# Seven block products instead of eight for half of the contraction in the gate and up projections

## The chip, the cores and the metric

The program runs on one core of a Trainium2 chip. The metric is the time of one execution on the device in microseconds. The kernel before took 1974.96 us, the median of three runs (1974.09 to 1976.55). About 0.2% of that, some 4 us, is what a measurement of this kernel can tell from no change.

Engines are named as in the profile: PE (TensorE, matrix products), PEld (its loads of the stationary operand), DVE (VectorE), ACT (ScalarE), POOL (GpSimd), SP (SyncE, which here only issues transfers). Each runs its own queue in order.

## What is computed

One decoder layer on 256 tokens of width 2048, all in float32: a SwiGLU half step, a mixer (dilated attention and gated linear attention), cross-attention into 256 memory tokens, and a second SwiGLU half step. The change concerns the two half steps:

```python
def swiglu(h, w_gate, w_up, w_down):
    return (jax.nn.silu(h @ w_gate) * (h @ w_up)) @ w_down
...
        x = x + 0.5 * swiglu(rms_norm(x, ffn1_norm[l]), ffn1_w_gate[l], ffn1_w_up[l], ffn1_w_down[l])
...
        x = x + 0.5 * swiglu(rms_norm(x, ffn2_norm[l]), ffn2_w_gate[l], ffn2_w_up[l], ffn2_w_down[l])
```

`w_gate` and `w_up` are 2048 x 5632, `w_down` is 5632 x 2048. The root-mean-square factor of a token is applied after the products, as a scale of a row; the gain vector is multiplied into the tokens before.

## The kernel before

**Three products for one.** TensorE multiplies float32r operands here. To keep float32 accuracy each operand is split exactly into two 12-bit parts, high and low, and a product becomes three: high times high, high times low, low times high (`mm3`, lines 130 to 136).

**Tiles.** The 256 tokens are two tiles of 128 (t = 0, 1). The contraction runs over 16 k tiles of 128, four of which make a group: a group of weights is 128 partitions x 4 x 512, one megabyte, one transfer. A chunk f is 512 columns of `w_gate` and of `w_up`; there are 11 chunks in a half step. A matrix product instruction has a 128x128 block of the tokens as its stationary operand and 512 weight columns as the moving one; the result adds into a PSUM bank of 128 x 512 (pool `acc`, four banks).

**Weights on their way.** `wgroup` (lines 108 to 127) loads a group into a buffer `raw` (three of them) from SP's queue, and hands it on in halves of two k tiles: ACT writes the high part `wh` (line 125), DVE the low part `wl = raw - wh` (line 126). There are four buffers each for `wh` and `wl` (`WB = 4`), so the split of a half can begin once PE has finished with the half four before it. `proj` (line 138) runs over the groups; each half feeds 12 matrix products, two k tiles x two token tiles x three.

**A chunk.** `ffn` (line 228): gate projection, then `sg = silu(r * acc)` on ACT (line 250), up projection, then `h = r * acc * sg` on DVE (line 256). `h` is transposed by PE into `tp` (line 239, eight transposes) and split again into `hTh`, `hTl` (lines 157 and 158). After all 11 chunks the down projection runs over four chunks of 512 output columns, each over all 11 groups.

**What sets the order.** The source is a Tile program: a scheduler puts the instructions of each engine into a fixed order when the program is built, by priority (weight splits have a raised one, `WPRI`) and by its own estimates, and derives all semaphores. `later(n, fn)` puts work off by n halves of a projection. Buffers come from pools; an instruction that needs a buffer waits until the last reader of its former content is done. In the pool `up` (`UB = 44` buffers of 2 KB per partition) lie the split h, and most tiles of the mixer.

## Time and profile before

| | |
|---|---|
| runs | 1974.96 us median of three, 1974.09 to 1976.55 |
| profiled execution, span | 1974.5 us; its page gives no other time of its own, and the span lies inside the range of the runs |
| one gate and up chunk (58.06 to 102.48 us) | 44.42 us |
| PE busy | 1966.5 us, 100% of the span |
| DVE busy | 1039.2 us, 53% |
| ACT busy | 912.3 us, 46% |
| POOL busy | 61.2 us, 3% |
| DMA engines | 52.2% busy for the queue of the loads, 370.74 MB |
| TensorE clock granted | 0.999 of full speed |

A busy share is the time in which at least one instruction of the engine was in execution; PE's instructions overlap, so that 0.39 us of one matrix product is not the time after which the next may start. An "idle before" is the time an engine stood still before instructions of a group, and the name behind the arrow is what ended it. The two half steps' gate and up chunks lie at 14 to 502 us and from about 1289 us on, each followed by a down projection; mixer and cross-attention lie between.

### The profile page before, as it was taken

Reading aid. Unit: us, or ns where it says so; the run is one execution under the profiler, and the core shown is the slowest. Engines: PE = TensorE matmul, PEld = TensorE weight load, DVE = VectorE, ACT = ScalarE, POOL = GpSimd, SP = SyncE. Lnnn points to the kernel's source line nnn. Section 1 sums busy time; section 2 is a strip of 40 time slices with the busy share of each in tenths; the row PEclk is TensorE's granted clock in tenths of the full one; section 3 lists DMA queues with packets and bytes.
Section 4 is the critical chain, followed back from the end, with each engine's and each line's share of the span. In section 5 each row is a group of like instructions: output and inputs, shape, how many; then the busy total and the mean of one; then the engine's idle time right before and its main releaser. Section 6 shows DMA issues by size and latency. Waiting matters only on the chain.

```text
span 1974.5 us, 22181 instructions
## 1 busy us (share of the span) xinstructions
PE 1966.5 (100%) x9000; PEld 1632.6 (83%) x9000; DVE 1039.2 (53%) x1102; ACT 912.3 (46%) x1115; POOL 61.2 (3%) x61
## 2 busy tenths in 40 slices
PE   9999999999999999999999999999999999999999
PEld 7888888888888888778888889888888888888887
DVE  6455444444455545546785566654444444444443
ACT  6444444444444436444576446544444444433332
POOL 2000000000000000002230000000000000000000
PEclk9999999999999999999999999999999999999999
DMA  8555555555555554445465554455555555555553
GB/s 308 187 191 189 192 192 192 187 188 187 189 190 190 195 204 149 171 156 201 172 219 204 196 186 154 173 192 192 188 187 188 188 189 190 191 192 202 203 204 116
DMA packets 57683, 374.26 MB, mean 190 GB/s; under 512 B 6475, under 2 KB 7627, under 8 KB 13932
## 3 DMA queue, kind: packets, MB, share of 16 engines
q1 hardware_dynamic: 56428, 370.74, 52.2%
q10 hardware_dynamic: 1152, 2.10, 0.3%
q8 instruction: 70, 1.15, 0.2%
q14 instruction: 33, 0.27, 0.0%
HBM read 370.72 MB, written 2.10 MB: 189 GB/s over the span
## 4 chain that ended last, share of the span: by engine, by line
PE 99%; DMA 0%; SPq 0%; DVE 0%; ACT 0%; POOL 0%; issue 0%; POOLq 0%
PE acc L136 32%; PE acc L134 32%; PE acc L135 32%; PE tp L239 1%; PE tp L198 1%; DMA xr<-in_xT_dram 0%; PE dsp L475 0%; PE op L492 0%; PE op L496 0%; PE tp L582 0%; PE sc L595 0%; PE op L629 0%; PE sc L738 0%; PE op L773 0%; PE tp L616 0%; PE zp L409 0%
## 5 line engine op out<-in xcount | busy, mean ns | idle before, releaser
L126 DVE TENSOR_TENSOR wl<-raw,wh 128x1024 fp32r<-128x1024 f32 (+1 forms) x690 | 845.6, 1227 | 855.5 <-ACT wh L125 855.1
L125 ACT CAST wh<-raw 128x1024 fp32r<-128x1024 f32 (+1 forms) x690 | 724.8, 1052 | 965.5 <-PE acc L136 944.6
L134 PE MATMUL acc<-wh,xTh 128*128 128x512 f32 x1824 | 714.8, 392 | 1.8 <-ACT wh L125 1.8
L135 PE MATMUL acc<-wl,xTh 128*128 128x512 f32 x1824 | 710.9, 390 | 1.0 <-DVE wl L126 1.0
L136 PE MATMUL acc<-wh,xTl 128*128 128x512 f32 x1824 | 710.7, 390 | 0.0
L134 PEld LDWEIGHTS acc<-wh,xTh 128*128 128x128 f32 x1824 | 342.5, 188 | 73.6 <-ACT wh L125 3.0
L135 PEld LDWEIGHTS acc<-wl,xTh 128*128 128x128 f32 x1824 | 343.0, 188 | 72.7 <-DVE wl L126 2.5
L136 PEld LDWEIGHTS acc<-wh,xTl 128*128 128x128 f32 x1824 | 342.8, 188 | 71.5
L134 PE MATMUL acc<-wh,hTh 128*128 128x512 f32 x704 | 274.3, 390 | 0.0
L136 PE MATMUL acc<-wh,hTl 128*128 128x512 f32 x704 | 273.9, 389 | 0.0
L135 PE MATMUL acc<-wl,hTh 128*128 128x512 f32 x704 | 273.9, 389 | 0.0
L136 PEld LDWEIGHTS acc<-wh,hTl 128*128 128x128 f32 x704 | 132.1, 188 | 27.5
L134 PEld LDWEIGHTS acc<-wh,hTh 128*128 128x128 f32 x704 | 132.1, 188 | 27.4
L135 PEld LDWEIGHTS acc<-wl,hTh 128*128 128x128 f32 x704 | 132.2, 188 | 27.2
L134 PE MATMUL acc<-wh,mTh 128*128 128x512 f32 x128 | 50.1, 392 | 0.0
L136 PE MATMUL acc<-wh,mTl 128*128 128x512 f32 x128 | 49.8, 389 | 0.0
L135 PE MATMUL acc<-wl,mTh 128*128 128x512 f32 x128 | 49.8, 389 | 0.0
L250 ACT ACTIVATE sg<-acc,r 128x512 f32<-128x512 f32 x44 | 30.1, 687 | 6.1 <-PE acc L136 6.1
L134 PE MATMUL acc<-wh,memh 128*128 128x256 f32 (+1 forms) x96 | 31.4, 327 | 0.0
L256 DVE SCALAR_TENSOR_TENSOR h<-acc,r,sg 128x512 f32<-128x512 f32 x44 | 30.9, 743 | 0.0
L136 PE MATMUL acc<-wh,meml 128*128 128x256 f32 (+1 forms) x96 | 30.6, 318 | 0.0
L135 PE MATMUL acc<-wl,memh 128*128 128x256 f32 (+1 forms) x96 | 30.5, 318 | 0.0
(249 smaller groups left out, 801.3 us busy)
## 6 DMA issues: line engine op xcount, KB each, us to landing
raw<-in_ffn_w_up_dram SPq DMA_DIRECT2D x88, 1024.0 KB, 4.8
raw<-in_ffn_w_down_dram SPq DMA_DIRECT2D x88, 1024.0 KB, 4.8
raw<-in_ffn_w_gate_dram SPq DMA_DIRECT2D x85, 1024.0 KB, 4.8
raw<-in_w_in_dram SPq DMA_DIRECT2D x48, 1024.0 KB, 4.8
raw<-in_w_out_dram SPq DMA_DIRECT2D x16, 1024.0 KB, 4.8
raw<-in_xattn_w_k_dram SPq DMA_DIRECT2D x4, 1024.0 KB, 4.7
raw<-in_xattn_w_q_dram SPq DMA_DIRECT2D x4, 1024.0 KB, 4.7
raw<-in_xattn_w_v_dram SPq DMA_DIRECT2D x4, 1024.0 KB, 4.9
```

What stands on the lines that cost most here:

```text
L125: SC.copy(wh[:, d], src)
L126: V.tensor_sub(wl[:, d], src, wh[:, d].bitcast(F32))
L134: PE.matmul(acc[t], lh, wh, start=first and i == 0, stop=False)
L135: PE.matmul(acc[t], lh, wl, start=False, stop=False)
L136: PE.matmul(acc[t], ll, wh, start=False, stop=last and i == len(half) - 1)
L198: PE.transpose(tp[:, j], src[:, t, j * P:(j + 1) * P], ident)
L239: PE.transpose(tp[:, j], hs[t][:, j * P:(j + 1) * P], ident)
L250: SC.activation(s, acc[t], AF.Silu, scale=r[:, t:t + 1])
L256: V.scalar_tensor_tensor(h, acc[t], r[:, t:t + 1], sg[t], op0=ALU.mult, op1=ALU.mult)
```

## The change

For 10 of the 11 chunks of each half step (all but f = 0), half of the contraction is done by seven block products instead of eight (`seven`, new). The 2 x 2 blocks are: the tokens' t = 0 and 1 by k-tile groups 0 and 1, times the weights' groups 0 and 1 by gate and up. The old way needs eight products of a token block (128 x 512) with a weight group (512 x 512): two tokens, two groups, two matrices. The new one has seven, each of 12 matrix products (four k tiles x three parts). Here they are P1 to P7 in program order, with the weight that each one splits:

- P1: gate group 0 + gate group 1 (`b11` after the first sum)
- P2: gate group 1 (`b21`)
- P3: gate group 0 + gate group 1 + up group 0 (`b11` after the second sum)
- P4: up group 1 (`b22`)
- P5: all four (`b11` after the third sum)
- P6: up group 0 (`b12`)
- P7: up group 0 + gate group 0 (`b12` after its sum)

Of the four weight sums two are made by a transfer that adds what it brings onto the buffer (`add_hbm`, issued from POOL's queue: `b11` before P1, `b12` between P6 and P7), two by DVE on the whole group of 128 x 2048 (`add`). Five differences of token blocks stand on the other side; they are made once in a half step (`differences`), on POOL, split by ACT and DVE. Intermediate sums are taken out of PSUM (`s21`, `s22`, `s12`: copies on ACT, and four additions or subtractions of 128 x 512 on DVE in a chunk). The other half of the contraction, groups 2 and 3, stays as it was (`plain`): U2 and U3 of up between P6 and P7, then G2 of gate, P7, G3. The halves of each are called a and b.

Every weight block of the seven is split anew, so that a chunk has 11 group splits instead of 8. All four PSUM banks of `acc` are in use during a chunk: Y, Z, X, R.

Buffers: `raw` five instead of three, `UB` 34 instead of 44, `SB` 8 instead of 6. So that 34 do, a half step is done in two segments, chunks 0 to 5 and 6 to 10, each with its own part of the down projection, which is added to the running x.

```diff
-UB = 44
-SB = 6
+UB = 34
+SB = 8
+RB = 5
+SEGS = (range(0, 6), range(6, NF))
...
-                raw = wp.tile([P, kn, n], F32, tag="raw", name="raw")
+                raw = wp.tile([P, kn, n], F32, tag="raw", name="raw", bufs=RB)
...
+    def parts(raw):
+        for h in range(2):
+            with tc.high_priority(WPRI):
+                wh = wp.tile([P, 2, 512], F32R, tag="wh", name="wh", bufs=WB)
+                wl = wp.tile([P, 2, 512], F32R, tag="wl", name="wl", bufs=WB)
+                src = raw[:, 2 * h:2 * h + 2]
+                SC.copy(wh, src)
+                V.tensor_sub(wl, src, wh.bitcast(F32))
+            yield [(2 * h + kk, wh[:, kk], wl[:, kk]) for kk in range(2)]
+
+    def add(dst, src):
+        with tc.high_priority(WPRI):
+            V.tensor_add(dst, dst, src)
+
+    def add_hbm(dst, src):
+        with tc.high_priority(WPRI):
+            G.dma_start(dst, src, accum_op=ALU.add)
+
+    def mms(bank, form, half, start, stop):
+        hi, lo = form
+        for i, (k, wh, wl) in enumerate(half):
+            PE.matmul(bank, hi[:, k], wh, start=start and i == 0, stop=False, skip_group_check=True)
+            PE.matmul(bank, hi[:, k], wl, start=False, stop=False, skip_group_check=True)
+            PE.matmul(bank, lo[:, k], wh, start=False, stop=stop and i == len(half) - 1, skip_group_check=True)
+
+    def product(bank, form, raw, start):
+        for h, half in enumerate(parts(raw)):
+            mms(bank, form, half, start and h == 0, h == 1)
+            tick()
+
+    def plain(banks, forms, raw, start, order):
+        for h, half in enumerate(parts(raw)):
+            for t in order:
+                mms(banks[t], forms[t], half, start[t] and h == 0, h == 1)
+            tick()
+
+    def differences():
+        x = {}
+        for c in range(2):
+            for t in range(TT):
+                x[t, c] = U([P, 4, P], F32, "xf")
+                hi, lo = (p[:, :, t * P:(t + 1) * P].bitcast(F32) for p in xT[c])
+                G.tensor_tensor(x[t, c], hi, lo, op=ALU.add)
+        r = {}
+        for name, a, b in (("22-21", (1, 1), (1, 0)), ("12-21", (0, 1), (1, 0)), ("22-12", (1, 1), (0, 1)),
+                           ("21-11", (1, 0), (0, 0)), ("11-12", (0, 0), (0, 1))):
+            d = W2([P, 4, P], "d")
+            G.tensor_tensor(d, x[a], x[b], op=ALU.subtract)
+            hi = U([P, 4, P], F32R, "Fh")
+            lo = U([P, 4, P], F32R, "Fl")
+            SC.copy(hi, d)
+            V.tensor_sub(lo, d, hi.bitcast(F32))
+            r[name] = (hi, lo)
+        return r
+
+    def seven(W1, W2_, f, F, A12, A21, rest):
+        Y, Z, X, R = [pa.tile([P, 512], F32, tag="acc", name="acc") for _ in range(4)]
+        b11 = load(W1, f, 0)
+        b21 = load(W1, f, 1)
+        add_hbm(b11, W1[f, 1])
+        product(Y, A21, b11, True)
+        s21 = W2([P, 512], "s21")
+        SC.copy(s21, Y)
+        b12 = load(W2_, f, 0)
+        product(Z, F["22-21"], b21, True)
+        add(b11, b12)
+        product(Y, F["12-21"], b11, False)
+        s22 = W2([P, 512], "s22")
+        SC.copy(s22, Y)
+        b22 = load(W2_, f, 1)
+        product(X, F["22-12"], b22, True)
+        add(b11, b22)
+        product(R, A12, b11, True)
+        V.tensor_sub(s22, R, s22)
+        product(Y, F["21-11"], b12, False)
+        add_hbm(b12, W1[f, 0])
+        s12 = W2([P, 512], "s12")
+        SC.copy(s12, Y)
+        for g in (2, 3):
+            plain((R, X), (rest(0, g), rest(1, g)), load(W2_, f, g), (False, False), (1, 0))
+        V.tensor_sub(s12, R, s12)
+        V.tensor_add(s22, X, s22)
+        plain((Y, Z), (rest(0, 2), rest(1, 2)), load(W1, f, 2), (False, False), (1, 0))
+        product(Y, F["11-12"], b12, False)
+        plain((Y, Z), (rest(0, 3), rest(1, 3)), load(W1, f, 3), (False, False), (0, 1))
+        V.tensor_add(s21, Z, s21)
+        return Y, s21, s12, s22
...
-        for f in range(NF):
-            acc = proj(wg, f, lhs_x, range(4), fine if f == 0 else None)
...
+        for seg in SEGS:
+            for f in seg:
+                if f == 0:
+                    acc = proj(wg, f, lhs_x, range(4), fine)
+                    if callable(r):
+                        r = r()
+                    F = differences()
+                else:
+                    y, s21, s12, s22 = seven(wg, wu, f, F, x_block(0, 1), x_block(1, 0), x_block)
+                    acc = [y, s21]
...
+            for c in range(NC):
+                acc = proj(wd, c, lhs_h, seg, last=last and final and c == NC - 1)
```

(`load`, also new, is the transfer of one group into a `raw` buffer from SP's queue, line 164 of the changed file.)

**DVE.** Line numbers of the rows below are those of each file; a row with x14 stands for 14 in a row. Before, from the middle of one chunk to the middle of the next:

```order
L126 TENSOR_TENSOR wl<-raw,wh 128x1024 x14
L256 SCALAR_TENSOR_TENSOR h<-acc,r_333,sg 128x512 x2
L126 TENSOR_TENSOR wl<-raw,wh 128x1024 x2
L158 TENSOR_TENSOR hTl<-tp,hTh 128x512 x2
L126 TENSOR_TENSOR wl<-raw,wh 128x1024 x14
```

Now, from the end of chunk 4 on. The first row's five splits are P7b, G3a and G3b of chunk 4 and P1a and P1b of chunk 5; then comes the first weight sum on DVE (L180), P2a, the addition from Z (L257), the first h (L372), P2b and P3a, the second h, P3b, the first split of the transposed h (L262), P4a and the second weight sum:

```order
L175 TENSOR_TENSOR wl<-raw,wh 128x1024 x5
L180 TENSOR_TENSOR raw<-raw 128x2048
L175 TENSOR_TENSOR wl<-raw,wh 128x1024
L257 TENSOR_TENSOR s_1541<-acc,s_1541 128x512
L372 SCALAR_TENSOR_TENSOR s_1653<-s_1653,r_333,sg 128x512
L175 TENSOR_TENSOR wl<-raw,wh 128x1024 x2
L372 SCALAR_TENSOR_TENSOR s_1586<-s_1586,r_333,s_1541 128x512
L175 TENSOR_TENSOR wl<-raw,wh 128x1024
L262 TENSOR_TENSOR hTl<-tp,hTh 128x512
L175 TENSOR_TENSOR wl<-raw,wh 128x1024
L180 TENSOR_TENSOR raw<-raw 128x2048
L175 TENSOR_TENSOR wl<-raw,wh 128x1024
```

Behind the last row (P4b) follow the other L262, eight splits (P5a to U3b), and the subtraction from R (L245), then G2a, G2b, P7a and the two sums of L253 and L252. What was two uneven splits around h is now a sequence with seven further instructions in it.

**PE.** The place in the changed chunk 2 at which U2 and U3 begin on bank R (`acc_847`), after 15 products of U2 and the first k tile of U3 into bank X (`acc_846`); wh_1007 is U2a, wh_1023 U2b, wh_1041 U3a:

```order
L191 MATMUL acc_846<-wh_1023,xTl2_223 128x512
L189 MATMUL acc_846<-wh_1041,xTh3_262 128x512
L190 MATMUL acc_846<-wl_1042,xTh3_262 128x512
L191 MATMUL acc_846<-wh_1041,xTl3_263 128x512
L189 MATMUL acc_847<-wh_1007,xTh2_222 128x512
L190 MATMUL acc_847<-wl_1008,xTh2_222 128x512
```

The fifth row adds into R, which the subtraction of L245 must have read before; of the halves U2a to U3a none is given back until its products into R are done. Before, a half's 12 products stood together.

**SP and POOL.** The loads in one changed chunk stand in SP's queue in this order (the first two rows are `b11` and `b21`, then `b12`, `b22`, U2, U3, G2, G3, and the next chunk's `b11`):

```order
L164 DMA raw_1173<-in_ffn1_w_gate_dram 128x2048
L164 DMA raw_1175<-in_ffn1_w_gate_dram 128x2048
L164 DMA raw_1218<-in_ffn1_w_up_dram 128x2048
L164 DMA raw_1263<-in_ffn1_w_up_dram 128x2048
L164 DMA raw_1330<-in_ffn1_w_up_dram 128x2048
L164 DMA raw_1364<-in_ffn1_w_up_dram 128x2048
L164 DMA raw_1400<-in_ffn1_w_gate_dram 128x2048
L164 DMA raw_1454<-in_ffn1_w_gate_dram 128x2048
L164 DMA raw_1498<-in_ffn1_w_gate_dram 128x2048
```

The five buffers are handed on in a fixed way: `b11` of a chunk takes the buffer of U2 of the chunk before, `b21` that of U3, `b12` that of G2, `b22` that of `b12`, U2 that of G3, U3 that of `b21`, G2 that of `b22`, G3 that of `b11`. Each load waits for the last split out of its buffer. POOL's queue holds the adding transfers alone through the chunks, in turn onto `b11` and `b12`; the one onto `b11` waits for the load of `b11`.

More of the change, by code (lines that the diff above doesn't have):

```diff
@@ L154, in proj, with load @@
         return acc
+    def load(W, c, g):
+        with tc.high_priority(WPRI):
+            raw = wp.tile([P, 4, 512], F32, tag="raw", name="raw", bufs=RB)
+            SY.dma_start(raw, W[c, g])
+        return raw
+    def parts(raw):
[7 more added lines that the diff above has]
+            yield [(2 * h + kk, wh[:, kk], wl[:, kk]) for kk in range(2)]
@@ L260, in lhs_h @@
         def lhs_h(k, t):
             return tuple(p[:, k % 4] for p in hT[k // 4, t])
-        for c in range(NC):
-            acc = proj(wd, c, lhs_h, range(NF), last=last and c == NC - 1)
-            for t in range(TT):
-                V.scalar_tensor_tensor(xs[c][:, t], acc[t], 0.5, xs[c][:, t], op0=ALU.mult, op1=ALU.add)
-            after(c)
+        for seg in SEGS:
[8 more added lines that the diff above has]
+                    acc = [y, s21]
+                sg = []
+                for t in range(TT):
+                    s = acc[t] if f and t else W2([P, 512], "sg")
+                    SC.activation(s, acc[t], AF.Silu, scale=r[:, t:t + 1])
+                    sg.append(s)
+                acc = [s12, s22] if f else proj(wu, f, lhs_x, range(4))
+                hs = []
+                for t in range(TT):
+                    h = acc[t] if f else W2([P, 512], "h")
+                    V.scalar_tensor_tensor(h, acc[t], r[:, t:t + 1], sg[t], op0=ALU.mult, op1=ALU.mult)
+                    hs.append(h)
+                later(1, lambda f=f, hs=hs: turn(f, hs))
+            final = seg is SEGS[-1]
+            for c in range(NC):
+                acc = proj(wd, c, lhs_h, seg, last=last and final and c == NC - 1)
+                for t in range(TT):
+                    V.scalar_tensor_tensor(xs[c][:, t], acc[t], 0.5, xs[c][:, t], op0=ALU.mult, op1=ALU.add)
+                if final:
+                    after(c)
```

19 lines of the change are left out of this document (4 added, 15 removed).

## The prediction

> **What bounds the kernel now.** I read the page first: busy times, then the chain of waits.
>
> ```profile
> span 1974.5 us, 22181 instructions
> PE 1966.5 (100%) x9000; PEld 1632.6 (83%) x9000; DVE 1039.2 (53%) x1102; ACT 912.3 (46%) x1115; POOL 61.2 (3%) x61
> PE 99%; DMA 0%; SPq 0%; DVE 0%; ACT 0%; POOL 0%; issue 0%; POOLq 0%
> ```
>
> PE alone sets the end: its own queue is 99% of the chain that ended last, so a matrix product less is time less as long as PE's operands stay ready. Next the stretches of single chunks, cut at PE's transposes of h, which stand once in a chunk, and the groups of instructions in the first stretch.
>
> ```profile
> core 0: us, PE busy (x) PEld busy (x) DVE busy (x) ACT busy (x) POOL busy (x), PEclk, DMA share, GB/s
> 58.06:102.48 44.42, 44.42 (x203) 36.87 (x201) 22.13 (x20) 19.13 (x20) 0.00 (x0) 1.00 0.53 189
> 1333.06:1377.48 44.42, 44.42 (x203) 36.87 (x201) 22.12 (x20) 19.12 (x20) 0.00 (x0) 1.00 0.53 190
> ...
> 58.06 0.87 PE tp L239 x8
> 102.48 0.87 PE tp L239 x8
> ...
> L126 DVE TENSOR_TENSOR wl<-raw,wh 128x1024 fp32r<-128x1024 f32 x16 | 19.6, 1225 | 22.3 <-ACT wh L125 22.3
> L125 ACT CAST wh<-raw 128x1024 fp32r<-128x1024 f32 x16 | 16.9, 1056 | 25.0 <-PE acc L136 25.0
> L256 DVE SCALAR_TENSOR_TENSOR h<-acc,r,sg 128x512 f32<-128x512 f32 x2 | 1.4, 744 | 0.0
> ```
>
> A chunk takes 44.42 us in both half steps at full clock and has 2 matrices x 16 k tiles x 2 token tiles x 3 parts = 192 products: (44.42 - 0.87) / 192 = 0.2268 us for one. DVE is busy for 22.1 us of it, ACT for 19.1. Both idle because they are ahead: ACT waits for PE to give buffers back, DVE for ACT.
>
> **The saving.** Seven blocks of 12 products in place of eight take 12 off a chunk, 20 chunks have it: 12 x 0.2268 = 2.72 us, times 20 = 54.4 us. PE's own work in a chunk is then 180 x 0.2268 + 0.87 = 41.70 us. Nothing is added to PE. That floor is 1974.5 - 54.4 = 1920.1 us.
>
> **The load on DVE.** It splits 11 groups in a chunk instead of 8, adds two whole groups, and does four sums of 128 x 512. Whether that is hidden needs the cost of one operation behind another. All group rows (the first two are of the whole span), then single instructions in order of time (start, duration):
>
> ```profile
> L126 DVE TENSOR_TENSOR wl<-raw,wh 128x1024 fp32r<-128x1024 f32 (+1 forms) x690 | 845.6, 1227 | 855.5 <-ACT wh L125 855.1
> L158 DVE TENSOR_TENSOR hTl<-tp,hTh 128x512 fp32r<-128x512 f32 x44 | 28.2, 682 | 0.0
> ...
> 883.89 2.35 DVE L126 TENSOR_TENSOR wl<-raw,wh 128x1024 fp32r<-128x1024 f32 x2
> 886.16 1.28 DVE L158 TENSOR_TENSOR mTl<-tp,mTh 128x512 fp32r<-128x512 f32 x2
> ...
> 99.30 1.40 DVE L256 SCALAR_TENSOR_TENSOR h<-acc,r,sg 128x512 f32<-128x512 f32 x2
> ```
>
> Two that are ready follow each other before the first has ended: a split takes 2.35 - 1.23 = 1.13 us of the queue, a 128 x 512 with one operand in PSUM 1.28 - 0.68 = 0.60, an h 1.40 - 0.74 = 0.66. A sum of 128 x 2048 is not in this trace: from 0.682 for 512 and 1.227 for 1024 columns each 512 more cost 0.545, so 1.227 + 2 x 0.545 = 2.32 us, 2.22 of the queue (an estimate). A chunk is 22 x 1.13 + 2 x 2.22 + 4 x 0.60 (sums) + 2 x 0.60 (split h) + 2 x 0.66 = 34.2 us out of 41.7: it fits, but not evenly. P1 to P6 are 16.3 us of products (72 x 0.2268) and want 12 splits, 13.6 us, and in the same stretch come both weight sums, both h and three other operations.
>
> **The cycle through DVE.** Only four halves can be split ahead, so DVE cannot fill its idle time of the plain groups with work for the next chunk. The tightest loop: PE ends P7b and gives its buffer to P1b; ACT casts it; DVE splits P1b and then works without a break up to the subtraction of L245; only then may PE add into R.
>
> ```profile
> 299.71 0.39 PE L136 MATMUL acc<-wh,xTl 128*128 128x512 f32 x1
> ...
> 300.14 1.05 ACT L125 CAST wh<-raw 128x1024 fp32r<-128x1024 f32 x1 [0.67 <-PE acc L136]
> ...
> 857.20 1.05 ACT L125 CAST wh<-raw 128x1024 fp32r<-128x1024 f32 x1 [3.83 <-PE acc L136]
> ...
> 858.28 1.23 DVE L126 TENSOR_TENSOR wl<-raw,wh 128x1024 fp32r<-128x1024 f32 x1 [2.58 <-ACT wh L125]
> ```
>
> - Release to split: the cast starts 0.43 us after the start of the last product, 0.20 after that product's turn of 0.227; the split starts 1.08 after the cast: 1.28 us.
> - DVE from P1b to L245: 15 splits (P1b to P6b without P1a are 11, U2 and U3 four) x 1.13 = 16.9; two weight sums 4.4; two h 1.3; sum from Z, two split h, L245: 4 x 0.60 = 2.4. Together 25.1, and 0.1 for the end of the last.
> - PE from its first product into R to the end of P7b: 69 products (both banks' rest of U2 and U3 33, G2 24, P7 12) x 0.2268 = 15.65.
>
> The sum is 42.1 us, 0.4 above PE's floor. A step on the way adds to it: P5 can only be cast after the second weight sum, and followed through from the end of a chunk with these durations PE stands 0.3 us for that cast and 0.4 for DVE's part of P5, after which L245 comes just in time. I take **42.4 us** a chunk. Against 44.42 that is 2.0 us, times 20 = **40 us**.
>
> The bounds for this term: at best DVE is never late, 41.7 us. At worst the operations do not overlap, since each waits for a semaphore: 15 x 1.227 + 2 x 2.32 + 2 x 0.744 + 4 x 0.682 = 27.3 in place of 25.2, and the cycle is 44.2.
>
> **The adding transfers.** SP has slack now, since it waits for buffers and not for landings:
>
> ```profile
> SPq L115 <- DVE wl L126: 1725.7, 333, 14.6
> ...
> raw<-in_ffn_w_gate_dram SPq DMA_DIRECT2D x85, 1024.0 KB, 4.8
> raw<-in_ffn_w_gate_dram SPq DMA_DIRECT2D x4, 512.0 KB, 8.1
> ```
>
> Such a transfer appears nowhere in the trace. Its window: the load of `b11` begins when U2b of the chunk before is split, about 18.3 us into a chunk by the same following of the queues (P2a's split begins 0.7 us before the chunk's first product; from there to U2b's end 12 splits, one weight sum and five small operations are 18.9 us). It lands 5 us later; the cast of P1a of the next chunk may begin 6.6 us before that chunk (P1a takes over P7a's buffer, and behind P7a stand P7b and G3, 30 products or 6.8 us, less 0.2 for the release). With 42.4 us a chunk that leaves 42.4 - 6.6 - 18.3 - 5.0 = 12.5 us. The one onto `b12` has from the split of P6b (16 us) to the cast of P7a at the latest (about 32): 16 us. What it costs: at least the 4.8 us of a plain load of the same megabyte; at most the rate of the crowded start, 8.1 us for half of one, 16.2 us. The nearest row is the plain load, which reads one operand where this reads two: twice that, 9.6 us. So hidden, with 3 us to spare. All transfers: 0.53 x 44.42 = 23.5 us of the DMA engines for 8 MB is 2.9 for one, and two more at 2.9 to 5.9 make 29 to 35 of 42.4 us, room enough on the mean.
>
> The Trainium skill, "Collectives: The Full Stack", section "The bandwidth ceiling: the fold count and why AG ≠ RS ≠ AR", says that a transfer that adds runs at half the rate of a copy because it reads two sources; by that the sum is unchanged, by a plain load's 4.8 us too. No run here shows it yet.
>
> **The rest.** The differences (nine POOL operations, 1.47 us each by the row below, and five splits) lie beside chunk 0, 43.6 us of PE with DVE half idle; uncovered they would be some 15 us twice. The eight additional sums into x in a half step, of 128 x 512 and so 0.68 us each, lie beside stretches of down projection of 27 to 33 us (120 or 144 products) whose next banks are free. The smaller pool `up` can only bite in the mixer, where the order of work is unchanged: 0. For the two new starts of a segment and the first chunks I add 1 us.
>
> **Sum**: 1974.5 - 40 + 1 = 1935; the median is 0.5 above the span, so **1936 us**.
>
> **The rivals.**
> - *PE's floor*, 1920: speaks for it that all 0.7 us of waiting is a sum of small estimates; against, DVE's 25 us in a row. Chance 0.18.
> - *DVE without overlap*: 44.2 a chunk, 20 x 0.2 = 4 us, about 1971, no change or barely faster. Against it the rows above at 883.89 and 99.30; for it that more of the new operations wait for PE or ACT. 0.10.
> - *Adding transfers late*: at 16.2 us the one onto `b11` lands 3.7 us late in every chunk, and as the loop runs on through P1, the first weight sum and U2b, every microsecond is paid: 46.1 a chunk, 20 x 1.7 = 34 us slower, about **2009**. It decides from 12.5 us, and above 14.5 the change loses. For it: both transfers, and the loads of `b21` and `b12`, share the engines. 0.16 for a loss, 0.08 for a part of it (12.5 to 14.5 us, 1937 to 1975).
> - *POOL's issue blocked by DVE*. POOL and DVE do slow each other here:
>
> ```profile
> L180 POOL TENSOR_TENSOR xr<-xr,gain 128x512 f32<-128x512 f32 x14 | 20.3, 1465 | 34.0 <-DMA xr<-in_memT_dram 19.6 <-DMA xr<-in_xT_dram 14.4
> 14.05 1.73 DVE L126 TENSOR_TENSOR wl<-raw,wh 128x1024 fp32r<-128x1024 f32 x1 [0.26 <-ACT wh L125]
> ```
>
> Beside POOL's multiplication a split takes 1.73 us instead of 1.23. If an issue on POOL holds up one split in this way, twice 0.5 us in a chunk, the loop is 43.4 and the time 1956. 0.05. In "SBUF — State Buffer", section "Who interferes with whom", the Trainium skill says that a two-operand DVE instruction from SBUF contends only with a POOL instruction that reads SBUF; by that this rival is void, and the row, where POOL reads, agrees.
>
> **How the numbers follow.** The forecast, DVE's loop at 41.9 to 43.4 us a chunk, 1924 to 1955, has 0.43. Faster by over 0.2% (4 us, what a measurement can tell): floor, forecast, blocked issue, most of partly late and half of no overlap: 0.77. Within: 0.07. Slower: 0.16. The range: below 1918 only if something I don't see helps; above, from the lost cases as far as 1984. That leaves some 0.15 above and little below.
>
> **What would show it.** One product stays at 0.227 us and DVE's busy time in a chunk goes from 22 to about 35 us. PE's idle time, near nothing now, should be 14 us in all, before P5 (DVE's `wl`, ACT's `wh`) and perhaps R. Wrong would be: chunks of 41.7 us with no idle PE; waits of ACT's `wh` for the adding transfer at P1 or P7, or a landing above 12 us; a weight sum above 2.5 us.

## The result: slower by 3.8%

The changed kernel took **2048.78 us** (median, 2046.21 to 2055.91) against 1975.61 beside it: ratio 1.0376, 95% interval 1.0357 to 1.0395. 1936 us was forecast, and the range ended at 1984. From the page of the changed kernel: its head, the chain of waits by engine, and the transfers of the `up` blocks and of POOL's queue (the last number is the median time from issue to landing).

```profile
span 2048.2 us, 22538 instructions
PE 1959.7 (96%) x8760; PEld 1606.2 (78%) x8760; DVE 1331.1 (65%) x1368; ACT 1061.1 (52%) x1305; POOL 127.7 (6%) x119
PE 70%; DMA 14%; DVE 9%; issue 5%; ACT 2%; POOL 1%; SPq 0%; ACTq 0%; POOLq 0%; DVEq 0%
...
raw<-in_ffn_w_up_dram SPq DMA_DIRECT2D x88, 1024.0 KB, 6.8
...
raw<-in_ffn_w_gate_dram POOLq DMA_DIRECT2D x40, 1024.0 KB, 10.9
```

240 products fewer are there (8760 of 9000), yet PE's busy time fell by only 6.8 us where 54.4 were removed, and 14% of the chain that ended last is a transfer, where it was 0% before. An adding transfer took 10.9 us in the median of both kinds, onto `b11` and onto `b12`, and a load of `up` 6.8 instead of 4.8. Who waited for these transfers, from the groups of waits (total, times, longest):

```profile
ACT wh L174 <- DMA raw<-in_ffn_w_gate_dram: 72.3, 16, 6.4
...
PE tp L343 <- DVE s L372: 62.3, 16, 4.1
```

Sixteen times ACT waited for a block, and sixteen times PE stood still in front of the transposes of h. One chunk of the chain of waits (start, duration; PE's own steps are left out) shows how the two belong together:

```profile
132.94 9.00 DMA raw<-in_ffn_w_gate_dram
...
142.49 11.70 DMA raw<-in_ffn_w_gate_dram
...
154.29 1.06 ACT wh L174
...
156.52 1.23 DVE wl L175
...
157.81 2.17 issue
...
161.80 0.67 DVE s L372
```

The load of `b11` takes 9.0 us, the adding transfer onto it 11.7; then come the cast and the split of P1, the weight sum (the 2.17 us are its time on DVE's queue), and behind it h (L372), for which the transposes of PE wait. From the start of the load to the cast of P1a that is 21.35 us. What PE did at that place, in order of time:

```profile
158.52 0.39 PE L189 MATMUL acc<-wh,xTh 128*128 128x512 f32 x1
158.74 0.39 PE L190 MATMUL acc<-wl,xTh 128*128 128x512 f32 x1
162.60 0.91 PE L343 MATMUL tp<-ident,s 128*128 128x128 f32 x4 [3.47 <-DVE s L372]
163.16 0.77 PE L191 MATMUL acc<-wh,xTl 128*128 128x512 f32 x1
163.74 0.63 PE L189 MATMUL acc<-wh,xTh 128*128 128x512 f32 x1
164.16 0.63 PE L190 MATMUL acc<-wl,xTh 128*128 128x512 f32 x1
...
166.27 0.40 PE L189 MATMUL acc<-wh,Fh 128*128 128x512 f32 x1
166.50 0.40 PE L190 MATMUL acc<-wl,Fh 128*128 128x512 f32 x1
```

PE is idle 3.47 us, and behind that the products start 0.43 us apart instead of 0.23 until 166.27; the clock that is granted to PE is one half in that time (shown below, with the experiment on the clock). The four products of P1 behind the transposes had their operands some 5 us earlier (the split of P1b began at 156.52), but in PE's fixed order they stand behind them. The starts of the subtraction from R (L245) give the time of a chunk: 47.4 to 50.0 us, 48.8 in the mean, where it was 44.42. (In the kernel before the first chunk of the second half step begins near 1240 us; 1289, said above, is where its h is transposed.)

### The profile page after: what moved, and what is told of

Its sections match the earlier page's. It is cut to its first block, busy times and chain, and to the rows that moved or that the text cites. A ratio compares the mean times of both kernels' runs of the same rounds, so it can differ in the third digit from the quotient of the medians.

```text
span 2048.2 us, 22538 instructions
## 1 busy us (share of the span) xinstructions
PE 1959.7 (96%) x8760; PEld 1606.2 (78%) x8760; DVE 1331.1 (65%) x1368; ACT 1061.1 (52%) x1305; POOL 127.7 (6%) x119
## 4 chain that ended last, share of the span: by engine, by line
PE 70%; DMA 14%; DVE 9%; issue 5%; ACT 2%; POOL 1%; SPq 0%; ACTq 0%; POOLq 0%; DVEq 0%
PE acc L136 16%; PE acc L138 16%; PE acc L137 16%; DMA raw<-in_ffn_w_gate_dram 13%; PE acc L191 6%; PE acc L189 6%; PE acc L190 6%; DVE wl L175 6%; ACT wh L174 2%; PE tp L343 1%; DVE raw L180 1%; DVE s L257 1%; DVE s L372 1%; DVE wl L128 0%; PE tp L302 0%
## 5 line engine op out<-in xcount | busy, mean ns | idle before, releaser
L128 DVE TENSOR_TENSOR wl<-raw,wh 128x1024 fp32r<-128x1024 f32 (+1 forms) x370 | 461.3, 1250 | 375.5 <-ACT wh L127 374.1
L175 DVE TENSOR_TENSOR wl<-raw,wh 128x1024 fp32r<-128x1024 f32 x440 | 523.5, 1221 | 259.7 <-ACT wh L174 256.2
L174 ACT CAST wh<-raw 128x1024 fp32r<-128x1024 f32 x440 | 453.8, 1051 | 358.1 <-PE acc L191 247.0
L127 ACT CAST wh<-raw 128x1024 fp32r<-128x1024 f32 (+1 forms) x370 | 386.7, 1048 | 443.4 <-PE acc L138 404.4
L189 PE MATMUL acc<-wh,xTh 128*128 128x512 f32 x800 | 318.3, 398 | 9.2 <-ACT sg L366 7.2
L190 PE MATMUL acc<-wl,xTh 128*128 128x512 f32 x800 | 316.9, 396 | 4.7 <-DVE wl L175 4.7
L191 PE MATMUL acc<-wh,xTl 128*128 128x512 f32 x800 | 321.3, 402 | 0.0
L136 PE MATMUL acc<-wh,xTh 128*128 128x512 f32 x544 | 214.8, 396 | 3.3 <-DVE x L913 1.6
L137 PE MATMUL acc<-wl,xTh 128*128 128x512 f32 x544 | 212.6, 391 | 3.0 <-DVE wl L128 3.0
L138 PE MATMUL acc<-wh,xTl 128*128 128x512 f32 x544 | 212.0, 390 | 0.7 <-DVE xTl L286 0.7
L189 PEld LDWEIGHTS acc<-wh,xTh 128*128 128x128 f32 x800 | 152.6, 191 | 48.8 <-ACT wh L174 11.0
L190 PEld LDWEIGHTS acc<-wl,xTh 128*128 128x128 f32 x800 | 152.6, 191 | 40.7 <-DVE wl L175 8.8
L191 PEld LDWEIGHTS acc<-wh,xTl 128*128 128x128 f32 x800 | 154.5, 193 | 31.1
## 6 DMA issues: line engine op xcount, KB each, us to landing
raw<-in_ffn_w_gate_dram POOLq DMA_DIRECT2D x40, 1024.0 KB, 10.9
```

What stands on the lines that cost most here:

```text
L127: SC.copy(wh[:, d], src)
L128: V.tensor_sub(wl[:, d], src, wh[:, d].bitcast(F32))
L136: PE.matmul(acc[t], lh, wh, start=first and i == 0, stop=False)
L137: PE.matmul(acc[t], lh, wl, start=False, stop=False)
L138: PE.matmul(acc[t], ll, wh, start=False, stop=last and i == len(half) - 1)
L174: SC.copy(wh, src)
```

## The experiments

**Theory A**: the chain of `b11`'s load and the adding transfer onto it is too long for its window. **Rival B**: DVE's work alone is too much, with or without adding transfers. Within A: the addition makes the transfer slow, or POOL's issuing does.

### Without adding transfers

```diff
-        add_hbm(b11, W1[f, 1])
...
-        add_hbm(b12, W1[f, 0])
```

> The changed kernel without its two adding transfers; DVE's and PE's order stay row for row. It leaves out two of the four weight sums (gate group 1 is missing in P1, P3 and P5, gate group 0 in P7), so that its output is not the layer's. Theory A (the loss is the chain load of b11, adding transfer onto b11, P1): without them nothing is late, the chunk falls from about 47.4 us to the 42.4 us of DVE's loop, 1936 us (1925 to 1950). Theory B (DVE's queue alone is too long, with or without the transfers): the chunk stays above 45 us and the time above 1990 us.

1956.09 us, ratio 0.9902 (0.9882 to 0.9922). From the table by stretches, one chunk:

```profile
core 0: us, PE busy (x) PEld busy (x) DVE busy (x) ACT busy (x) POOL busy (x), PEclk, DMA share, GB/s
171.00:213.65 42.65, 42.58 (x190) 34.27 (x189) 35.16 (x33) 26.42 (x30) 0.00 (x0) 1.00 0.55 198
```

A chunk is 42.65 us, PE is busy in all of it, and DVE's 35.2 us do not stop it. B falls: 92.7 us of the changed kernel's time go with the two transfers. But 20 chunks of 42.65 instead of 44.42 would be 35 us less than before, and the span is only 19.5 less. The other 16 us lie outside the steady chunks, and for them the time lies above the 1925 to 1950 us that I expected.

### The sum onto b11 by DVE

```diff
-        add_hbm(b11, W1[f, 1])
+        add(b11, b21)
```

> The first weight sum (b11 + b21 before P1) is made by DVE from the two loaded groups instead of by an adding transfer; the one onto b12 stays. Theory A: b11 needs one landing instead of two in a row, and the load of b11 no longer has an adding transfer behind it; the transfer onto b12 has some 16 us and takes 11 to 12, so it stays hidden. DVE's additional 2.2 us lie before P1, where it stands idle: 42.4 to 43 us a chunk, 1936 to 1950 us. Theory B: DVE gets 2.2 us more in each of 20 chunks, 2048 + 44 = 2092 us.

1963.2 us, ratio 0.9938 (0.9923 to 0.9953): the same layer, 0.6% faster than before, but not the 1936 to 1950 us expected. The adding transfer onto `b12`, now alone, took 9.2 us:

```profile
L180 DVE TENSOR_TENSOR raw<-raw 128x2048 f32<-128x2048 f32 x60 | 137.4, 2290 | 49.2 <-DMA raw<-in_ffn_w_gate_dram 48.5
...
raw<-in_ffn_w_gate_dram POOLq DMA_DIRECT2D x20, 1024.0 KB, 9.2
```

DVE's weight sums (2.29 us each) wait 49 us in all for blocks. These waits cost little: chunks last 42.6 to 43.6 us, apart from the first and the last of a segment.

### The same transfers from POOL's queue, without the addition

```diff
-            G.dma_start(dst, src, accum_op=ALU.add)
+            G.dma_start(dst, src)
```

> The two transfers of POOL's queue write instead of adding, with the same bytes, the same waits, the same buffers and the same order on every engine. It leaves out two of the four weight sums (each is replaced by its second summand). Theory A1 (the addition makes the transfer slow): they land after 5 to 7 us, the load of b11 after 6 instead of 9, so that b11 is ready in time: 1936 to 1950 us. Theory A2 (issuing from POOL's queue makes it slow, by its descriptors): they still land after 10 us or more, and the time stays near 2040 us.

1957.36 us, ratio 0.9908 (0.9888 to 0.9928). Every engine has the same order as in the changed kernel; only the addition is gone. The issues on POOL and the landing:

```profile
L184 POOL DMA_DIRECT2D raw<-in_ffn_w_gate_dram x40 | 21.6, 539 | 1085.8 <-DVE wl L175 702.8 <-DVE wl L128 265.9 <-DMA raw<-in_ffn_w_gate_dram 97.4
...
raw<-in_ffn_w_gate_dram POOLq DMA_DIRECT2D x40, 1024.0 KB, 5.2
```

5.2 us instead of 10.9, 0.54 us of POOL for an issue instead of 0.87, and chunks of 42.6 us (the time misses my 1936 to 1950 by the same loss outside the chunks). So the addition makes the transfer long, not the queue it comes from, nor the order of work.

### Segments and buffers alone

```diff
-                if f == 0:
-                    acc = proj(wg, f, lhs_x, range(4), fine)
+                if True:
+                    acc = proj(wg, f, lhs_x, range(4), fine if f == 0 else None)
```

(and the up projection by `proj` in every chunk too; `SEGS` and the buffers as changed.)

> Only the buffers and the two segments of the change: all chunks by eight block products as before, five raw buffers, 34 instead of 44 in the pool up, down projection in two parts. Theory A: this costs nothing, 1975 us within 4. Rival C (a part of the loss lies in the segments or in the smaller pool): 1980 us or more.

1975.61 us, ratio 1.0000 (0.9990 to 1.0009): they cost nothing.

### Do the two adding transfers spoil one another?

The transfer onto `b12` runs while the next `b11` is loaded. Here it is out and the one onto `b11` stays:

```diff
-        add_hbm(b12, W1[f, 0])
```

> The change with the adding transfer onto b12 taken out and the one onto b11 kept (one of the four weight sums is left out, its product uses b12 alone). In the changed kernel the chain in a chunk is b11's load (9.0 us) and then the adding transfer onto it (11.7 us), 20.7 us together, against a window of 17.5 us from the split that starts the load to the product that needs the sum. Theory C, the two adding transfers spoil one another (b11's load runs beside the transfer onto b12): without b12's, the load falls to 5 to 7 us and the transfer to about 9.2 (what it took in the run with one alone), 14 to 16 us together, inside the window; chunks of 42.6 to 43.5 us, 1955 to 1970 us in all. Theory D, the transfer onto b11 alone is too long: load and transfer stay near 9 and 11 us, the first product still waits about 3.5 us in most chunks, 2010 to 2045 us.

1957.61 us, ratio 0.9911 (0.9893 to 0.9929), chunks of 42.6 us, no wait in front of the transposes.

```profile
raw<-in_ffn_w_up_dram SPq DMA_DIRECT2D x88, 1024.0 KB, 5.0
...
raw<-in_ffn_w_gate_dram POOLq DMA_DIRECT2D x20, 1024.0 KB, 9.3
...
128.69 0.33 SPq L164 DMA_DIRECT2D raw<-in_ffn_w_gate_dram  x1
...
146.28 1.06 ACT L174 CAST wh<-raw 128x1024 fp32r<-128x1024 f32 x1 [0.30 <-PE acc L191]
```

Theory C holds. The load of `b11` (issued at 128.69) lands within 5.3 us instead of 9.0, the transfer onto it, issued at 133.98, takes 8.6, and the cast of P1a at 146.28 waits for PE and no longer for the block. From the load's issue to that cast are 17.6 us: this is the window.

The two adding transfers never run at the same time, though. In the chunk of the changed kernel shown above the one onto `b12` goes out here and lands after 9.8 us, at 140.75, before the one onto `b11` goes out at 142.49:

```profile
130.93 0.86 POOL L184 DMA_DIRECT2D raw<-in_ffn_w_gate_dram  x1 [35.32 <-DVE wl L175]
```

Over the 20 chunks the one onto `b12` took 8.9 to 11.0 us, 9.35 in the median, hardly more than alone; the one onto `b11` 9.1 to 14.4, 12.2 in the median. So the first spoils the load of `b11` beside it, and by that the second goes out later, when loads of `up` are under way. In the trace's packets its data begin to move 4.3 us after the issue (median), where it is 1.6 us in the version with this transfer alone; the moving then takes 8.3 us against 6.9. That it waits for the plain loads issued shortly before it is likely, but not shown by itself.

### All four sums by DVE

```diff
-        add_hbm(b11, W1[f, 1])
+        add(b11, b21)
...
-        add_hbm(b12, W1[f, 0])
+        add(b12, load(W1, f, 0))
```

> The same layer with all four weight sums by VectorE and no adding transfer: b11+b21 from the two blocks in SBUF, b12+b11 from a further plain load of b11. VectorE gets two sums of 2.29 us more in each chunk than in the changed kernel, 25.1+4.6 us of work in its loop. Theory A (the adding transfers alone made the change slow): far under 2049 us. If each sum lengthens the loop in full, 42.6+2x2.29 = 47.2 us a chunk, above the 44.4 of before: 1956+20x4.6 = 2048 us. If each costs what the sum onto b11 cost in the run with one (1963.2-1956.1 = 7 us in all), 1956+14 = 1970 us. I expect the second, 1965 to 1985 us, with the shorter chunk ends taken up by VectorE's idle time.

1977.91 us, ratio 1.0015 (1.0006 to 1.0024): my 1965 to 1985 held, and the gain is gone.

```profile
171.00:214.73 43.73, 42.89 (x189) 34.20 (x188) 39.41 (x36) 26.45 (x30) 0.00 (x0) 1.00 0.58 217
```

Each chunk is 43.73 us (the columns are those above): 4.58 us more of DVE made it 1.1 longer.

### No sums at all

Is the 42.65 DVE's loop of the prediction (42.4), or does PE itself need it? The two sums that stay with DVE in the change are left out too:

```diff
-        add(b11, b12)
-        product(Y, F["12-21"], b11, False)
+        product(Y, F["12-21"], b12, False)
...
-        add(b11, b22)
-        product(R, A12, b11, True)
+        product(R, A12, b22, True)
```

> The version without adding transfers, in which the two weight sums of VectorE are left out as well (so all four are missing: the products take b12, b22 and the other blocks alone). VectorE's continuous stretch in a chunk, from the split of P1b to the subtraction of L245, becomes 4.4 us shorter. Theory L, VectorE's loop of the prediction sets the 42.6 us a chunk of the versions without a late transfer: chunks fall to TensorE's 41.7 us (180 products and 8 transposes), 20 x 0.9 = 18 us less than 1956, 1936 to 1942 us. Theory P, the 0.9 us above 41.7 is TensorE's own (transposes in two parts, products to other banks between), and the loop is shorter than forecast: chunks stay at 42.5 to 42.7 us, 1948 to 1957 us, the little gain from the first chunk alone.

1933.7 us, ratio 0.9788 (0.9771 to 0.9805).

```profile
171.00:212.90 41.90, 41.90 (x189) 34.49 (x188) 31.41 (x30) 26.67 (x30) 0.00 (x0) 1.00 0.55 201
```

Chunks fall to 41.90 us, 0.2 above PE's floor of 41.70: theory L, though the time lies 2 us under its range: of the 22 us gained 15 are the chunks', the rest lies outside them. The two sums cost 0.75 us a chunk. In the version with them this is no idle time of PE that a table of waits names; in the chunk shown above it is seven places at which a product or the transposes start 0.1 to 0.2 us late, 0.9 us in all, against three and 0.3 us here.

### Does the idle time lower the clock?

Ten products that nobody reads, ahead of the transposes of h; eight of them landed right in front of the place where PE had waited:

```diff
+            if f:
+                fill = PM([P, 512], "tp")
+                for _ in range(10):
+                    PE.matmul(fill, xT[0][0][:, 0, 0:P], xT[0][0][:, 0:2], start=True, stop=True)
```

> The changed kernel with ten products of 128x512 more in each of the 20 chunks of seven products, which read only x and whose result nobody reads; eight of them stand right ahead of the transposes at which TensorE was idle 3.4 to 4.1 us in 16 chunks, 8x0.227 = 1.8 us. Theory, that an idle time of this length lowers the granted clock (7 or so products at 0.43 us behind it): the idle time falls to 1.6 to 2.3 us, the slow products go, and each chunk becomes about 1.5 us shorter although it does more: about 2025 us, 2010 to 2035. Rival, that the clock falls for another reason (mean load, or the other engines): slow products stay, and the time is 2045 to 2060 us.

2068.82 us, ratio 1.0475 (1.0461 to 1.0489): the time missed my 2025, and the theory's count of what it would save fell. The waits before the transposes are still 54.8 us in all (62.3 before), presumably since PE gives back the buffers on which the next load of `b11` depends in the end: work put into PE would delay the chain, too. That is argued, not shown. What the fill did change are the lengths of the waits, and these sort the slow products. In order of time, behind a wait of 2.08 us:

```profile
114.64 0.63 PE L347 MATMUL tp<-ident,s 128*128 128x128 f32 x4 [2.08 <-DVE s L376]
115.34 0.39 PE L190 MATMUL acc<-wl,xTh 128*128 128x512 f32 x1
115.57 0.40 PE L191 MATMUL acc<-wh,xTl 128*128 128x512 f32 x1
```

Full pace at once. I counted this over the waits of 0.4 us and more between 39 and 900 us, in the changed kernel and all versions told here. A slow product is one that starts over 0.36 us before its successor, in the 7 us behind a wait. All 19 waits of 3.3 to 7.8 us had 5 to 12 of them; of the ten from 2.3 to 2.8 us, eight had 5 to 11 and two had none; of the shorter ones, apart from those that fall into the 7 us behind a longer wait, none had more than one, except a pair of 1.23 and 0.76 us close together (in the version with x early, below), which had eight. Where there were more than one they cost 1.1 to 2.7 us in all. So the length of a wait alone does not decide. The granted clock does: in these traces it is 1.00 or 0.50, and within a trace it changes only at times that lie a multiple of 3.41 us apart. I call a stretch of 3.41 us between two such times a frame. Stretches cut at these times, two waits of the version with the fill and then the chunk of the changed kernel shown above (PEclk is the third number from the end):

```profile
208.46:211.87 3.41, 1.72 (x8) 1.10 (x6) 3.41 (x4) 0.46 (x1) 0.00 (x0) 1.00 0.01 2
211.87:215.28 3.41, 1.79 (x9) 1.26 (x9) 3.41 (x5) 2.14 (x3) 0.00 (x0) 1.00 0.13 19
...
484.93:488.35 3.42, 0.94 (x7) 0.65 (x6) 3.42 (x5) 1.39 (x2) 0.00 (x0) 1.00 0.00 0
488.35:495.18 6.83, 6.10 (x18) 4.45 (x17) 4.83 (x7) 2.86 (x5) 0.00 (x0) 0.50 0.44 156
...
159.39:162.80 3.41, 0.20 (x2) 0.23 (x3) 3.41 (x5) 0.97 (x2) 0.00 (x0) 1.00 0.00 0
162.80:166.22 3.42, 3.42 (x11) 2.81 (x10) 2.61 (x3) 2.19 (x3) 0.00 (x0) 0.50 0.38 117
```

A wait of 2.57 us falls into two frames, PE is busy for about half of either, and the clock stays. One of 2.48 us falls into a single frame, PE is busy for 0.94 us of it, and the next two frames have half the clock. Over all traces, from 18 us on: behind each of the 44 frames at full clock in which PE was idle for 1.95 us or more the clock fell, and behind two of the 37 with 1.0 to 1.94 us (1.67 and 1.85). So idle time does lower the clock, counted by the frame; this explains the pair of short waits, too. That removing the slow products alone would shorten the changed kernel by their sum is not shown.

### The first chunk

In the faster versions some 10 us are lost at the start. Seven stretches of 15 us from the span's start, summed, of the kernel before:

```profile
sum 105.00, PE 101.14 PEld 82.51 DVE 58.91 ACT 56.60 POOL 11.25; mean PE 14.45 PEld 11.79 DVE 8.42 ACT 8.09 POOL 1.61
```

and of the version with `b11`'s transfer alone:

```profile
sum 105.00, PE 91.32 PEld 72.80 DVE 77.21 ACT 60.29 POOL 28.44; mean PE 13.05 PEld 10.40 DVE 11.03 ACT 8.61 POOL 4.06
```

PE is busy 9.8 us less. Three edits on the version with `b11`'s sum by DVE, one on top of the other. First, the differences earlier:

```diff
-                    if callable(r):
-                        r = r()
-                    F = differences()
+                    with tc.high_priority(40):
+                        F = differences()
+                    if callable(r):
+                        r = r()
```

(with `d` in the pool `up`.)

> The version with b11's sum by VectorE (1963.2 us), in which the five differences of x blocks stand ahead of the layer's r1 and 40 places earlier in the order, with buffers of the other pool. In that version TensorE stood idle 2.30 us (sg) and 4.14 us (Fl) in the first chunk of seven products, and ran 8 to 10 products at 0.43 us instead of 0.23 after each. Theory: the differences, queued behind weight splits and a weight sum, are the cause: the 4.14 us and the slow products behind them go, about 6 us, 1955 to 1959 us. Rival: the first chunk is late because GpSimd's work slows VectorE's splits (2.1 us each beside it instead of 1.22), which stays: 1961 to 1965 us.

1963.73 us, as without it (1963.2): the theory fell. PE's two waits became one of 6.44 us, for `sg`. From SyncE's queue:

```profile
30.61 9.64 SPq L164 DMA_DIRECT2D raw<-in_ffn_w_gate_dram  x2
43.40 0.33 SPq L164 DMA_DIRECT2D raw<-in_ffn_w_up_dram  x1
43.77 0.43 SPq L435 DMA_DIRECT2D x<-in_x_dram  x1
```

The last load of x, on which the layer's r1 and so `sg` depend, stands behind loads that wait for a buffer. So x was put ahead of them:

```diff
-            with tc.high_priority(XPRI - 34 * c):
+            with tc.high_priority(XPRI + 40 - 34 * c):
```

> The version with b11's sum by VectorE and the early differences (1963.7 us), with the four loads of x ahead of all loads of the seven products' blocks in SyncE's queue. In that version the fourth x load is issued at 43.8 us, behind loads that wait for a buffer; the layer's r1 comes at 65 us, the activation that gives TensorE its bank at 66, and TensorE stood idle 6.44 us and then ran 6 products at 0.43 us. Theory: with x early the 6.4 us and the 1.4 us behind them go, 7 to 8 us less: 1955 to 1957 us. Rival: the weights that are now behind x come late and TensorE waits as long for them in chunk 0: 1961 to 1965 us.

1962.89 us: no change again. The 6.4 us are gone and were lost earlier instead, the rival's way. Two stretches of it, then DVE's groups between 15 and 45 us:

```profile
15.00:30.00 15.00, 12.02 (x49) 8.45 (x47) 15.00 (x9) 5.77 (x7) 14.22 (x9) 1.00 1.03 422
30.00:45.00 15.00, 11.48 (x41) 8.46 (x42) 12.92 (x12) 10.62 (x19) 7.67 (x5) 0.89 0.72 285
...
L128 DVE TENSOR_TENSOR wl<-raw,wh 128x1024 fp32r<-128x1024 f32 x10 | 16.0, 1628 | 0.5 <-ACT wh L127 0.5
L221 DVE TENSOR_TENSOR Fl<-d,Fh 128x512 fp32r<-128x512 f32 x5 | 6.5, 1336 | 0.0
```

In the first of the two DVE was busy without a break beside POOL's 14.2 us, and the operations on it were slow. So the differences went from POOL to DVE:

```diff
-                G.tensor_tensor(x[t, c], hi, lo, op=ALU.add)
+                V.tensor_tensor(x[t, c], hi, lo, op=ALU.add)
...
-            G.tensor_tensor(d, x[a], x[b], op=ALU.subtract)
+            V.tensor_tensor(d, x[a], x[b], op=ALU.subtract)
```

> The version with b11's sum by VectorE, early differences and early x (1962.9 us), with the nine operations that make the five differences on VectorE instead of GpSimd (some 0.6 us of its queue each, 5.4 us). In that version TensorE was busy 12.0 and 11.5 us of the stretches from 15 to 30 and 30 to 45 us, where it was 14.2 and 15.0 in the kernel before; VectorE was busy without a break there, beside 14.2 and 7.7 us of GpSimd, and its splits of 128x1024 took 2.1 us where they take 1.22 alone. Theory, GpSimd's work beside VectorE's costs the start: splits at 1.3 to 1.7 us again, TensorE at least 13.5 us busy in either stretch, 4 to 6 us less: 1957 to 1959 us. Rival, the start is short of VectorE or of transfers whoever makes the differences: 1961 to 1966 us.

**1955.66 us**, ratio 0.9902 (0.9886 to 0.9919), the fastest version that computes the whole layer: 1.0% below the kernel before. The same two stretches and groups:

```profile
15.00:30.00 15.00, 13.69 (x59) 10.86 (x60) 15.00 (x16) 8.32 (x13) 6.15 (x4) 1.00 1.03 422
30.00:45.00 15.00, 14.91 (x66) 11.96 (x65) 12.73 (x16) 12.01 (x21) 0.00 (x0) 1.00 0.95 371
...
L128 DVE TENSOR_TENSOR wl<-raw,wh 128x1024 fp32r<-128x1024 f32 x12 | 14.9, 1263 | 0.4 <-ACT wh L127 0.4
...
L221 DVE TENSOR_TENSOR Fl<-d,Fh 128x512 fp32r<-128x512 f32 x5 | 3.4, 689 | 2.1 <-ACT Fh L220 2.1
```

With nine operations more DVE is done sooner: a split takes 1.26 us in place of 1.63, an `Fl` 0.69 in place of 1.34, and PE is busy 28.6 us of the 30 instead of 23.5. The gain of 7.2 us is above the 4 to 6 expected.

### The kinds of sum exchanged

On the version with x early, `b11`'s adding transfer back and `b12`'s sum by DVE:

```diff
-        add(b11, b21)
+        add_hbm(b11, W1[f, 1])
...
-        add_hbm(b12, W1[f, 0])
+        add(b12, load(W1, f, 0))
```

> As the one before, with the two kinds of sum exchanged: the adding transfer onto b11 stays, and b12's sum is made by VectorE from a further plain load of b11. With b11's adding transfer alone and b12's sum left out the time was 1957.6 us with chunks of 42.6 us and 7.2 us of idle time before the first one, so 1950 us is the bound if the sum on b12 is hidden behind the plain groups, where VectorE waits for the casts. If it costs half of what both sums cost in the run with four (chunks of 43.74 against 42.63, 1.1 us), 20 x 0.55 = 11 us more: 1961 us. I expect 1950 to 1957 us, and no idle time for b11's sum, since its load has no other adding transfer beside it.

2019.75 us (2006.97 to 2039.22), ratio 1.0214 (1.0188 to 1.0241): far outside the 1950 to 1957 us expected. Ten of the steady chunks last 43.7 to 44.6 us, six others 46 to 50, and twelve times ACT waits for the block again. The adding transfer takes 9.8 us in the median, and its issue and the subtraction from R stand like this in one chunk:

```profile
136.78 0.68 DVE L245 TENSOR_TENSOR s<-acc,s 128x512 f32<-128x512 f32 x1
...
142.06 0.86 POOL L184 DMA_DIRECT2D raw<-in_ffn_w_gate_dram  x1 [43.39 <-DVE wl L175]
```

In the version with `b11`'s transfer alone, the same two:

```profile
130.85 0.68 DVE L245 TENSOR_TENSOR s<-acc,s 128x512 f32<-128x512 f32 x1
...
133.98 0.86 POOL L184 DMA_DIRECT2D raw<-in_ffn_w_gate_dram  x1 [41.92 <-DMA raw<-in_ffn_w_gate_dram]
```

The issue comes 5.3 us behind the subtraction instead of 3.1. One load more in each chunk also hands the five buffers on in another way; that this is why the chain starts later is argued, not shown. In the chunk shown the block comes only 0.6 us late. The six long chunks are those whose transfer took 11.4 to 12.9 us; in the ten others it took 9.2 to 10.1. So an adding transfer can become too long with no second one near it, and 2 us more decide.

## Why the prediction was wrong

**The step that failed** is "hidden, 3 us to spare". From the start of `b11`'s load to the cast of P1a I gave 5.0 us to the load and 12.5 to the window, 17.5 together, and needed 14.6. Measured were 9.0 and 11.7, with the steps between 21.35, that is 3.85 too late, and PE's idle time at that place is 3.4 to 4.1 us. The window was right (17.6 in the version with `b11`'s transfer alone), both terms in it too short. 9.6 us for the adding transfer is right for one alone (9.2 and 9.3), the load's 5 us for one without an adding transfer beside it (5.3). I knew the order on POOL's queue, one onto `b12` and then one onto `b11`, and had `b12`'s window of 16 us; I did not lay the two on one axis, where `b12`'s transfer (from 130.93 to 140.75) runs just as `b11` is loaded (from 132.94), and the transfer onto `b11` among the loads of `up`. The average I checked instead, 29 to 35 of 42.4 us of the DMA engines, says nothing of that place.

**The rival that came true** was "adding transfers late", at 0.16. Its mechanism and its decisive place were right, and so was "every microsecond is paid". Its price was too low: 46.1 us a chunk and 2009 us, against 48.8 and 2049. Against the version without adding transfers the changed kernel lost 92.7 us. PE's waits in front of the transposes in the sixteen late chunks are 62.3; the slow products behind the idle time, 1.1 to 2.3 us in each, some 25 more. The slow products were in no part of the prediction. The remaining 5 us are not traced; 4.7 us of short waits of PE for splits may be among them.

**The saving.** 12 x 0.2268 us a chunk was right: without any sums a chunk takes 41.90 us, against a floor of 41.70.

**The load on DVE.** A weight sum takes 2.29 us (2.32 estimated), and operations that are ready overlap. DVE's loop was to give 42.4 us: measured 42.65 with the change's two sums on DVE and no transfer late, and 41.90 with the sums out. Its form was not quite right, so that the near hit is in part luck. I expected 14 us of idle PE before P5 and R and there is next to none, only short late starts; and of the two further sums in the version with four, one lies inside that stretch and would lengthen my loop by 2.2 us, yet both together cost 1.1. So the loop as I added it up has about a microsecond of slack that I did not see. (A split's 2.35 - 1.23 is 1.12 us, not 1.13; this is 0.2 us in the loop.)

**The rest, 1 us.** Segments and the pools cost nothing, as said. The differences were to be hidden, "DVE half idle". But in chunk 0 DVE is not half idle between 15 and 30 us, where the kernel before kept it busy 14.7 of 15 us, and POOL's work slowed it there. About 10 us went at the start; with the differences on DVE and x early 7 of them came back. I had the row that shows this (a split of 1.73 us beside POOL's multiplication) and used it on the wrong rival, POOL's *issues*. Those cost nothing: in the version with `b11`'s transfer alone chunks took 42.6 us with POOL's 0.86 us of issue in each, and without it too.

**The chances.** Faster had 0.77. The sum of the parts that were right, 1956 to 1964 us, would have been faster; one overlap of transfers was enough to turn it.

Three rules of the Trainium skill bear on this. "Collectives: The Full Stack", section "The bandwidth ceiling: the fold count and why AG ≠ RS ≠ AR", gives the reducing steps of a ring collective half the rate of its copying ones, because an addition reads two sources: 9.3 against 5.2 us from the same queue, a factor of 1.8, is near it, for a transfer that runs alone. "SBUF — State Buffer", section "Who interferes with whom": a DVE instruction with two inputs from SBUF contends with POOL instructions that read SBUF; the splits of 1.63 us beside POOL's sums and 1.26 without these agree. "TensorE: Matmul & The Clock Gate", section "What's actually happening", lets the clock fall to one half after an idle window of about 3.4 us; the pace, 0.43 us against 0.227, agrees, but here 1.95 us of idle time within one frame of 3.41 us were enough.

## What to carry to other kernels

Price a transfer at the moment at which it runs: put it beside the transfers that the same few buffers release at that time, and add the durations along the whole chain (load, adding transfer, cast, split) before calling it hidden; a mean share of the DMA engines does not show a collision. A block sum that an engine with gaps can make in 2.3 us is safer than an adding transfer of 9 to 14 us, as long as its time falls into the gaps. When work is given to an idle engine, look at what it slows: taking nine operations onto the busy DVE was faster than leaving them on POOL beside it.

## What the runs showed of the hardware

- An adding transfer of one megabyte from HBM took 9.2 to 9.3 us in the median of two versions with one in a chunk, and 9.8, at most 12.9, in one with a plain load more beside it; in the changed kernel 9.35 onto `b12` and 12.2 (up to 14.4) onto `b11`, whose data begin to move only 4.3 us after the issue instead of 1.6. A plain one from the same queue took 5.2. The issue takes POOL 0.87 us, the plain one's 0.54.
- Plain loads beside it take longer: that of `b11` 9.0 us instead of 5.3 in the chunks shown, those of `up` 6.8 instead of 4.8 in the median.
- PE at full pace runs products 0.227 us apart. The granted clock changes only on a grid of 3.41 us. Behind every frame of it with 1.95 us or more of idle PE (44 of 44) it fell to one half for one or more frames, and products ran 0.43 us apart; behind frames with 1.0 to 1.94 us of idle time it fell twice in 37.
- Two-operand work on POOL lengthens DVE's two-operand work in SBUF beside it: 128x512 from 0.69 to 1.34 us, 128x1024 from 1.26 to 1.63 in the mean of a stretch of 30 us, 2.3 at the worst.
